# Rotation by 90 degrees: store sizes at the start and at the end of the store stretch

One core of a Trainium2 chip. The metric is the device time of one execution in microseconds (us). MB in the kernel's sizes means 1,048,576 bytes; GB/s and the bytes of the profile are decimal.

## The reference

```python
def reference(x):                       # x: (32, 3, 256, 256) float32
    return np.rot90(x, k=-1, axes=(-2, -1)).astype(np.float32)
```

Each of the 96 images of 256 x 256 numbers is turned clockwise. 25.17 MB are read and 25.17 MB are written; there is no arithmetic.

## The kernel before

The images are handled in 12 slabs of 2 MB. All of the input fits on the core, so each slab has a buffer of its own (`units[n]`), and slab n is turned into the buffer of slab n - 1, whose content is used up by then. Slab 0 has no predecessor: it is turned into `turned0` in PSUM and copied back to the last buffer at the end by ScalarE. VectorE does all the turning, two transposes for each slab; all transfers are issued from one queue, that of the sync engine (SP). The line numbers of the profile refer to the lines marked here.

```python
    for n in range(n_slabs):            # all 24 loads of 1 MB are issued first
        for i in range(I):              # I = 2
            if n in (0, last):
                nc.sync.dma_start(out=units[n][:, i], in_=ld8_v[n][:, i])            # L63
            else:
                nc.sync.dma_start(out=units[n][i::I]..., in_=ld16_v[n, i])           # L65

    for n in range(n_slabs):
        t_in, t_out = units[n], units[n - 1] if n else turned0
        if n in (0, last):
            for i in range(I):
                ...                     # each transpose makes one half of the slab
                nc.vector.transpose(out=dst[:, :, ::-1, ::-1], in_=src)              # L73
        else:
            for h in range(2):          # each transpose writes into both halves
                ...
                nc.vector.transpose(out=dst[:, cs], in_=src[:, cs])                  # L79

        if n == 1:                      # 128 KB, 896 KB, 1 MB
            nc.sync.dma_start(out=st_v[n][:, 0, :W], in_=t_out[:, 0, :W])            # L82
            nc.sync.dma_start(out=st_v[n][:, 0, W:], in_=t_out[:, 0, W:])            # L83
            nc.sync.dma_start(out=st_v[n][:, 1], in_=t_out[:, 1])                    # L84
        elif n in (2, 3):
            for i in range(I):
                nc.sync.dma_start(out=st_v[n][:, i], in_=t_out[:, i])                # L87
        elif n:
            nc.sync.dma_start(out=st_v[n], in_=t_out)                                # L89

    for i in range(I):
        nc.scalar.copy(out=units[last][:, i], in_=turned0[:, i])                     # L92
    nc.sync.dma_start(out=st_v[0], in_=units[last])                                  # L93
```

## Time and profile before

| | before |
|---|---|
| median of the first 3 runs | 123.54 us (123.51 to 123.78) |
| span of the profiled execution | 122.3 us |
| DMA queue, share of the 16 engines' span | 97.8% |
| rate in most slices | 429 GB/s |
| VectorE busy | 93.3 us (76%) |
| last transfer issued | 101.27 us |

VectorE's 76% looks high, but it ends at about 99 us while the transfers go on for another 21 us. Look at the chain that ended last, on the page of the kernel before (share of the span by engine, then by line):

```profile
DVE 47%; issue 27%; DMA 4%; DVEq 3%; ACT 2%
DVE u L79 37%; DVE turned L73 6%; DMA u<-in_x_dram 4%; DVE u L73 3%; DVEq L119 3%; ACT u L92 2%
```

It gives VectorE nearly half of the span and the transfers 4%.

### The profile page before, as it was taken

The numbers are of one execution on the slowest core, as the hardware profiler recorded it, in microseconds if no ns is written. First come the engines' busy times: TensorE is split into PE (matmuls) and PEld (weight loads), VectorE is DVE, ScalarE is ACT, GpSimd is POOL, SyncE is SP. The second block draws the span as 40 slices with busy tenths as digits, with TensorE's granted clock in tenths as the row PEclk, the third lists the DMA queues.
The fourth block names the chain that finished last, engine by engine and source line by source line (L and its number), as shares of the span: only waits on it lengthen the run. The fifth ranks groups of instructions, "written<-read, shape, count | busy, mean of one in ns | idle before, by whom it ended". The sixth has DMA issues, their size and how long they took to land.

```text
span 122.3 us, 138 instructions
## 1 busy us (share of the span) xinstructions
DVE 93.3 (76%) x24; ACT 5.0 (4%) x3; POOL 0.2 (0%) x4
## 2 busy tenths in 40 slices
DVE  0199999999999999999999999999999940000000
ACT  0000000000000000000400000000000641000000
POOL 0000000000000000000000000000000000000000
DMA  3999999999999999999999999999999999999994
GB/s 118 418 450 429 429 429 429 429 429 429 429 429 429 429 429 429 429 429 391 359 413 429 429 429 426 429 421 429 429 429 429 429 429 429 429 429 426 429 429 180
DMA packets 5632, 50.33 MB, mean 412 GB/s; under 512 B 640, under 2 KB 768, under 8 KB 896
## 3 DMA queue, kind: packets, MB, share of 16 engines
q1 hardware_dynamic: 5632, 50.33, 97.8%
HBM read 25.17 MB, written 25.17 MB: 412 GB/s over the span
## 4 chain that ended last, share of the span: by engine, by line
DVE 47%; issue 27%; DMA 4%; DVEq 3%; ACT 2%
DVE u L79 37%; DVE turned L73 6%; DMA u<-in_x_dram 4%; DVE u L73 3%; DVEq L119 3%; ACT u L92 2%
## 5 line engine op out<-in xcount | busy, mean ns | idle before, releaser
L79 DVE STREAM_TRANSPOSE u<-u 128x2048 f32<-128x2048 f32 x20 | 78.0, 3949 | 0.3
L73 DVE STREAM_TRANSPOSE turned<-u 128x2048 f32<-128x2048 f32 x2 | 7.6, 3828 | 5.6 <-DMA u<-in_x_dram 5.6
L73 DVE STREAM_TRANSPOSE u<-u 128x2048 f32<-128x2048 f32 x2 | 7.7, 3953 | 0.0
L92 ACT COPY u<-turned 128x2048 f32<-128x2048 f32 x2 | 3.7, 1866 | 36.5 <-DVE u L73 36.5
L92 ACT ACT_TABLE_LOAD x1 | 1.3, 1283 | 59.7 <-DMA u<-in_x_dram 59.7
L108 POOL MEMSET const-bfloat16-1.0<- 128x1 bf16 x1 | 0.1, 102 | 0.0
L108 POOL MEMSET const-uint8-127<- 128x1 uint8 x1 | 0.1, 102 | 0.0
L108 POOL MEMSET const-float32-0.0<- 128x1 f32 x1 | 0.1, 99 | 0.2 <-issue 0.2
L108 POOL MEMSET const-float32-1.0<- 128x1 f32 x1 | 0.1, 99 | 0.0
## 6 DMA issues: line engine op xcount, KB each, us to landing
u<-in_x_dram SPq DMA_DIRECT2D x24, 1024.0 KB, 19.6
out_dram<-u SPq DMA_DIRECT2D x9, 2048.0 KB, 23.0
out_dram<-u SPq DMA_DIRECT2D x5, 1024.0 KB, 17.7
out_dram<-u SPq DMA_DIRECT2D x1, 896.0 KB, 17.8
out_dram<-u SPq DMA_DIRECT2D x1, 128.0 KB, 18.3
```

What stands on the lines that cost most here:

```text
L73: nc.vector.transpose(out=dst[:, :, ::-1, ::-1], in_=src)
L79: nc.vector.transpose(out=dst[:, cs], in_=src[:, cs])
L92: nc.scalar.copy(out=units[last][:, i], in_=turned0[:, i])
L108: nc = _bacc.Bacc("TRN2", target_bir_lowering=False, num_devices=1)
L119: with _tile.TileContext(nc) as tc:
```

## The change

Large stores where the store stretch begins, small ones where it ends, with the number of transfers kept at 40. The likely intent: 2 MB stores carry less handling, and halves at the end can start as soon as their data is ready, so that less is left when the last piece of computing is over.

```diff
-        elif n in (2, 3):
+        elif n == last:
             for i in range(I):
                 nc.sync.dma_start(out=st_v[n][:, i], in_=t_out[:, i])
         elif n:
@@
     for i in range(I):
         nc.scalar.copy(out=units[last][:, i], in_=turned0[:, i])
-    nc.sync.dma_start(out=st_v[0], in_=units[last])
+        nc.sync.dma_start(out=st_v[0][:, i], in_=units[last][:, i])
```

## The prediction

> **What bounds the kernel now.** I read the page first, its rows for the 40 slices and for the DMA queue, because the kernel has no arithmetic beyond moving data:
>
> ```profile
> DMA  3999999999999999999999999999999999999994
> GB/s 118 418 450 429 429 429 429 429 429 429 429 429 429 429 429 429 429 429 391 359 413 429 429 429 426 429 421 429 429 429 429 429 429 429 429 429 426 429 429 180
> ...
> q1 hardware_dynamic: 5632, 50.33, 97.8%
> HBM read 25.17 MB, written 25.17 MB: 412 GB/s over the span
> ```
>
> The 16 DMA engines are busy for 97.8% of the span and move 429 GB/s in nearly every slice, loads first, stores after. 50.33 MB at 429 GB/s is 117.3 us. The span is 122.3 us, so only 5.0 us can be lost anywhere. The same row says where. A slice is 122.3/40 = 3.06 us. Slices 0 and 1 fall short by (311 + 11)/429 of a slice, 2.3 us, the start. Slices 18 to 20 (391, 359, 413), where the last loads give way to the first stores, fall short by (38 + 70 + 16)/429 of a slice, 0.9 us. The last slice falls short by 249/429 of one, 1.8 us, the end. That is all of it: 117.3 + 2.3 + 0.9 + 1.8 = 122.3 us. The kernel is bound by the transfers. The chain of waits on the page names VectorE with 47%, and is misleading here: it follows dependencies back from the last instruction, and a queue that is merely full isn't a dependency.
>
> Second, the timeline of the end, to see when work is ready and when it is issued (columns: start, length, engine, line, operation, names, count):
>
> ```profile
> 87.66 3.91 DVE L79 STREAM_TRANSPOSE u<-u 128x2048 f32<-128x2048 f32 x1
> 91.59 8.15 SPq L89 DMA_DIRECT2D out_dram<-u  x2
> 91.60 7.75 DVE L73 STREAM_TRANSPOSE u<-u 128x2048 f32<-128x2048 f32 x2
> 95.60 1.87 ACT L92 COPY u<-turned 128x2048 f32<-128x2048 f32 x1 [34.62 <-DVE u L73]
> 99.38 1.87 ACT L92 COPY u<-turned 128x2048 f32<-128x2048 f32 x1 [1.92 <-DVE u L73]
> 101.27 0.37 SPq L93 DMA_DIRECT2D out_dram<-u  x1
> ```
>
> The reader is to see that all computing is over at 101.25 us and the very last transfer is issued at 101.27 us, 21 us before the end. What happens in those 21 us, in windows (columns: stretch, its length, busy time of DVE, ACT and POOL, clock, DMA share, GB/s):
>
> ```profile
> 67.60:77.40 9.80, 9.73 (x4) 0.00 (x0) 0.00 (x0) 1.00 1.01 426
> 77.40:87.20 9.80, 9.77 (x3) 0.00 (x0) 0.00 (x0) 1.00 1.01 428
> ...
> 106.80:116.60 9.80, 0.00 (x0) 0.00 (x0) 0.00 (x0) 1.00 1.01 428
> 116.60:120.00 3.40, 0.00 (x0) 0.00 (x0) 0.00 (x0) 1.00 1.01 429
> 120.00:121.20 1.20, 0.00 (x0) 0.00 (x0) 0.00 (x0) 1.00 0.46 191
> ```
>
> The queue drains a backlog at full rate up to 120.0 us, ebbs away within about 1 us, and then come the final waits. The two slabs of the first window (67.6 to 77.4) are the ones stored in four 1 MB pieces; the next windows hold 2 MB stores. Both run at the same rate, 426 against 428.
>
> Third, the waits of the DMA queue, to see what paces the issues:
>
> ```profile
> SPq L65 <- DMA u<-in_x_dram: 25.5, 13, 2.0
> SPq L89 <- DVE u L79: 20.7, 4, 7.4
> ...
> SPq L87 <- DMA u<-in_x_dram: 8.3, 4, 2.1
> ```
>
> The four 1 MB stores that the change merges (L87) did not wait for VectorE. They waited for loads to land. From issue to landing the page gives 19.6 us for a load, and 1.049 MB at 429 GB/s takes 2.44 us: 8 transfers are in flight, and each issue waits for the transfer eight before it. The waits of L65 have the same form.
>
> **What the Trainium skill says.** "DMA: Bandwidth & Descriptors", section Where 436 GB/s comes from, puts the ceiling of a core's 16 DMA engines at 435 GB/s; the trace agrees, 429 sustained. The same page, Rules for kernel authors, asks for at least 1 MiB per DMA for full bandwidth. Every store that the change touches is 1 or 2 MB before and after, so both sides of it satisfy the rule, and the trace shows no difference between the two sizes. "Perfetto Trace Analysis", section DMA Optimizations, says of splitting: "If DMA engines are generally idle, splitting DMAs into smaller sections may allow the overall task to complete sooner." Here they are not idle at the place where the change splits, so its condition is not met.
>
> **The change part by part.**
>
> (a) Slabs 2 and 3: four stores of 1 MB become two of 2 MB. Removed: two issues of 0.33 us on the sync queue (timeline: 332 ns each), which lie beside a full queue and cost nothing. Bytes and rows of 8 KB stay as they are. Rate: if 426 against 428 were real and not the cut of the windows, it would be worth 0.5% of 9.8 us, 0.05 us. Both halves of such a slab become ready together (each transpose of L79 writes into both halves), so merging delays nothing.
>
> (b) Numbering. With two fewer stores early, every store of slabs 4 to 10 is issued one or two places further forward in the window of eight. Its data decides then: the waits of L89 for VectorE. Slabs 4 to 6 go out a few us sooner, into a queue that is already full. Cost and gain 0.
>
> (c) Slab 11: one 2 MB store becomes two of 1 MB. The first half is ready when the first L73 transpose ends, at about 95.5 us in place of 99.35 us. But when does the queue get to it? The bytes end at about 120.7 us; slabs 11 and 0 are the last two, 2.097 MB / 429 GB/s = 4.89 us each. So slab 11 begins to move at about 110.9 us and slab 0 at 115.8 us. Slab 11 has been ready for 11.5 us by then. Earlier by 3.9 us in the queue is later by nothing at the end: gain 0.
>
> (d) Slab 0: the same. Its second half is ready at 101.25 us as before, its first at 97.5 us but behind slab 11 in program order, so issued at about 99.8 us. Slack until 115.8 us: 14.5 us. Gain 0. The two extra issues, 0.33 us each, lie within the slack.
>
> (e) The window at the end. Forty transfers before and after. The last waits for the 32nd: before that was the store of slab 4, after it is that of slab 6. Stores start landing at about 62.7 us, so slab 6 lands at about 62.7 + 6 x 4.89 = 92 us, 9 us before the 40th wants to issue at 101.3 us. No new wait.
>
> (f) The end itself: the last transfer is 1 MB, not 2 MB. The ebb of about 1 us is the spread of the 16 engines, and they run through the same descriptors. I put 0.0, give or take 0.1 us.
>
> Sum: 0 with about 0.1 us either way, 123.5 us.
>
> **The rivals.**
>
> *Transition.* The dip of 0.9 us at slices 18 to 20 lies just where stores begin, and larger stores could help or worsen it. For it: the issues of slabs 2 and 3 (52.3 to 60 us) lie there. Against: the transfers that actually move then are the last loads and the three pieces of slab 1, which don't change. Were all of it won, 122.65 us; doubled, 124.4 us.
>
> *Queue room.* One 2 MB issue at 68.08 us took 2.31 us on the sync queue where others take 0.37 (timeline of the queue), so the queue seems to have a limit of outstanding work. With 2 MB stores from slab 2 on, this stall will come earlier, in the stretch from 57 to 68 us. If a stalled issue held back transfers, each would cost up to 2 us and the time would be 124 to 126 us. Against: in the stretch of the 2.31 us stall the DMA engines kept their 429 GB/s, since the stall means that the queue is full.
>
> *False dependency at the end.* If the second copy of ScalarE had to wait until the first half store of slab 0 has landed (about 118.5 us, the same tile), then 1.87 us of copy, some 2.4 us of transfer and the start of a transfer come after it: about 126 to 127 us. Against: the halves of a tile are kept apart already; the first copy runs at 95.60 us while VectorE still reads the other half of that tile (91.60 to 99.35 us).
>
> *A faster end.* The tail being the bound, earlier halves would win up to 3.8 us, 119.7 us. The 21 us of backlog after the last issue speak against it.
>
> **Range and chances.** The three runs before lie between 123.51 and 123.78 us. Predicted 123.5 us; the range 123.1 to 124.0 us holds this scatter, a few tenths of the transition either way, and a chip a little different. Two per cent are 2.5 us. Only the first rival can win anything and it can't win as much; faster 0.01. The false dependency or stacked stalls could lose it; slower 0.02. Same 0.97.
>
> **What would show it.** In the profile of the changed kernel: DMA share near 97.8% and 429 GB/s in all slices but the same three places; the sync queue's waits for VectorE moved to earlier stores; long issues (over 1 us) in the stretch 57 to 68 us without a dip beside them; the first half of slab 11 issued near 95.6 us and the last transfer still near 101.3 us, 20 us before the end. I am wrong if ScalarE's second copy starts later than about 100 us, if slices 18 to 22 change by more than a few per cent, or if the rate falls below 429 while the queue has work.

## The result, and the profile after

The changed kernel took 123.93 us (median of 6 runs, 123.80 to 124.30). The kernel before, with three runs more beside it, took 123.85 us (median of 6, 123.51 to 124.09). The ratio is 1.0016 with a 95% interval of 0.9993 to 1.0038: the same. Even that 0.16% hangs on the first three runs of the kernel before (mean 123.61 us): its three later runs have a mean of 123.99 us, the changed kernel's six one of 124.00 us. Two more sets of runs gave 0.9986 and 1.0002.

The page of the changed kernel, its DMA rows (busy tenths and GB/s in 40 slices, then the queue):

```profile
DMA  3999999999999999999999999999999999999994
GB/s 78 426 445 429 429 429 440 418 429 434 424 429 429 429 429 429 429 429 413 389 405 426 429 429 429 429 429 429 429 426 429 429 429 426 426 429 426 429 429 174
...
q1 hardware_dynamic: 5632, 50.33, 97.9%
```

The picture is the old one: 429 GB/s nearly everywhere, and less at the start, in slices 18 to 20 and at the end. The dip in the middle is somewhat shallower than before (413, 389, 405 against 391, 359, 413) and the start somewhat worse (78 against 118). Those two differ between executions of one and the same kernel, and here they nearly cancel.

The end of the changed kernel in its timeline (start, length, engine, line, operation, names, count):

```profile
91.75 0.37 SPq L89 DMA_DIRECT2D out_dram<-u  x1
91.75 7.75 DVE L73 STREAM_TRANSPOSE u<-u 128x2048 f32<-128x2048 f32 x2
95.75 4.13 SPq L87 DMA_DIRECT2D out_dram<-u  x2
95.75 1.87 ACT L92 COPY u<-turned 128x2048 f32<-128x2048 f32 x1 [34.82 <-DVE u L73]
99.54 1.86 ACT L92 COPY u<-turned 128x2048 f32<-128x2048 f32 x1 [1.92 <-DVE u L73]
99.97 2.49 SPq L93 DMA_DIRECT2D out_dram<-u  x2
```

The change does what it was meant to do. The first half of slab 11 is issued at 95.75 us, where the whole slab used to wait until 99.38 us. The second copy starts at 99.54 us, right after its transpose, so it waits for no store. It buys nothing, because the queue is busy with older work; here are the windows of the same trace after the last issue (stretch, length, busy time of DVE, ACT and POOL, clock, DMA share, GB/s):

```profile
106.70:116.50 9.80, 0.00 (x0) 0.00 (x0) 0.00 (x0) 1.00 1.01 428
116.50:119.90 3.40, 0.00 (x0) 0.00 (x0) 0.00 (x0) 1.00 1.01 426
119.90:121.10 1.20, 0.00 (x0) 0.00 (x0) 0.00 (x0) 1.00 0.46 191
```

Full rate to 119.9 us and about 1.2 us of ebbing away, as before.

And here is the chain that ended last on the page of the changed kernel:

```profile
DMA 52%; DVE 16%; issue 10%; DVEq 3%; ACT 2%; SPq 0%
DMA u<-in_x_dram 38%; DMA out_dram<-u 14%; DVE u L79 13%; DVE u L73 3%; DVEq L119 3%; ACT u L92 2%; SPq L63 0%; SPq L83 0%
```

From VectorE 47% to DMA 52% at the same time. It isn't the change that did this: two later profiles of the same changed kernel have DVE 47% with DMA 4%, and DVE 40% with DMA 20%. With 20 us of work in the queue, small differences seem to decide which dependency the chain follows back (argued, not tested). Neither version is a measurement of what bounds the kernel; the rate of the queue is.

### The profile page after: what moved, and what is told of

It is laid out like the page before. It is cut to its first block, busy times and chain, and to the rows that moved or that the text cites. A ratio compares the mean times of both kernels' runs of the same rounds, so it can differ in the third digit from the quotient of the medians.

```text
span 122.2 us, 140 instructions
## 1 busy us (share of the span) xinstructions
DVE 93.5 (76%) x24; ACT 5.0 (4%) x3; POOL 0.2 (0%) x4
## 3 DMA queue, kind: packets, MB, share of 16 engines
q1 hardware_dynamic: 5632, 50.33, 97.9%
## 4 chain that ended last, share of the span: by engine, by line
DMA 52%; DVE 16%; issue 10%; DVEq 3%; ACT 2%; SPq 0%
DMA u<-in_x_dram 38%; DMA out_dram<-u 14%; DVE u L79 13%; DVE u L73 3%; DVEq L119 3%; ACT u L92 2%; SPq L63 0%; SPq L83 0%
## 5 line engine op out<-in xcount | busy, mean ns | idle before, releaser
L73 DVE STREAM_TRANSPOSE turned<-u 128x2048 f32<-128x2048 f32 x2 | 7.6, 3829 | 5.7 <-DMA u<-in_x_dram 5.7
L73 DVE STREAM_TRANSPOSE u<-u 128x2048 f32<-128x2048 f32 x2 | 7.8, 3954 | 0.0
```

## The experiments

Theory: the transfers bound both kernels, 1 MB and 2 MB stores run at one rate, and the last slabs are ready some 10 us before the queue gets to them. So each part of the change is worth nothing, and only a drained queue would make the halves worth something.

Rivals: a part costs or wins a little, and the other hides it; the turn from loads to stores depends on store sizes; stalled issues hold transfers back; the end hangs on VectorE after all.

Beyond the first comparison there were 18 runs, of 14 kernels, all with correct results. The ratio is always to the kernel before in the same set.

| run | ratio | 95% interval | median us |
|---|---|---|---|
| after_again | 0.9986 | 0.9970 to 1.0002 | 123.66 |
| after_third | 1.0002 | 0.9988 to 1.0016 | 123.71 |
| merge_only | 1.0021 | 1.0003 to 1.0040 | 124.12 |
| merge_again | 1.0022 | 1.0006 to 1.0038 | 123.91 |
| merge_third | 1.0012 | 0.9999 to 1.0025 | 123.79 |
| tail_only | 1.0015 | 1.0000 to 1.0030 | 124.02 |
| tail_again | 1.0007 | 0.9992 to 1.0022 | 123.87 |
| before_again | 1.0005 | 0.9990 to 1.0020 | 123.82 |
| all_1mb | 1.0010 | 0.9990 to 1.0031 | 124.16 |
| all_2mb | 1.0014 | 0.9998 to 1.0031 | 123.86 |
| table_early | 1.0002 | 0.9987 to 1.0017 | 123.71 |
| late2_before | 0.9994 | 0.9978 to 1.0011 | 123.58 |
| late2_after | 1.0011 | 0.9995 to 1.0026 | 123.78 |
| late3_before | 1.0360 | 1.0333 to 1.0388 | 128.30 |
| late3_after | 1.0155 | 1.0128 to 1.0181 | 125.76 |
| late5_before | 1.1573 | 1.1538 to 1.1609 | 143.32 |
| late5_after | 1.1383 | 1.1367 to 1.1399 | 140.75 |
| late5_order | 1.1262 | 1.1232 to 1.1292 | 139.48 |

### The whole change, and each part alone

after_again and after_third are the changed kernel. The parts are small edits of the kernel before.

```diff
 merge_only:
-        elif n in (2, 3):
-            for i in range(I):
-                nc.sync.dma_start(out=st_v[n][:, i], in_=t_out[:, i])
 tail_only:
-        elif n in (2, 3):
+        elif n in (2, 3, last):
 ...
-    nc.sync.dma_start(out=st_v[0], in_=units[last])
+        nc.sync.dma_start(out=st_v[0][:, i], in_=units[last][:, i])
```

> The changed kernel once more, beside the two parts of its change. Theory (the transfers bound both kernels and every touched store waits in a full queue): ratio to the kernel before within 0.997 to 1.003. Rival (the two extra issues and the smaller pieces at the end cost a little, as the first measurement of 1.0016 hints): ratio above 1.0015 with an interval that leaves out 1.

> Only slabs 2 and 3 merged to one 2 MB store each, 38 transfers. Theory: ratio 0.997 to 1.003, 0 us. Rival (2 MB stores near the turn from loads to stores help or hurt there): up to 0.9 us either way, ratio 0.993 or 1.007, shown by slices 18 to 22.

> Only the last two slabs split in halves, 42 transfers. Theory: ratio 0.997 to 1.003, because the halves wait more than 10 us in the queue. Rival (an earlier start of the last stores shortens the end): 2.4 to 3.8 us less, ratio about 0.97 to 0.98. Rival (two more transfers cost their handling): 0.2 to 0.6 us more.

In this first set the parts lay at 1.0021 and 1.0015 with intervals at or just above 1, and the whole at 0.9986. Parts that cost 0.2% each can't make a whole that is faster, unless they undo each other. So the parts ran again, beside the kernel before against itself:

> The kernel before against itself. Theory (ratios of 0.998 to 1.002 here are scatter): it strays from 1 by up to 0.002, perhaps with an interval that nearly leaves out 1. Rival (the parts have a true cost): within 0.0005 of 1, with the repeated parts at 1.0015 to 1.002 beside it.

> The merge of slabs 2 and 3 alone, repeated. Theory: no fixed sign, 0.998 to 1.002. Rival (a true cost of 0.2%): 1.0015 to 1.0025 again.

> The split of the last two slabs alone, repeated. Theory: no fixed sign, 0.998 to 1.002. Rival (a true cost of 0.15%): 1.001 to 1.002 again.

The kernel before against itself gave 1.0005, the split alone 1.0007. But the merge gave 1.0022 again, against what I expected of scatter. So the merge and the whole change ran side by side once more:

> The merge alone a third time. If it has a true cost: 1.0015 to 1.0025. If scatter: anywhere from 0.998 to 1.002, and not apart from the changed kernel beside it by more than 0.002.

> The changed kernel a third time. Theory (no effect): 0.998 to 1.002. If the split gives back what the merge costs: 0.999 to 1.001 while the merge alone stands at 1.0015 to 1.0025.

1.0012 and 1.0002, intervals overlapping. The whole change is worth nothing: 1.0016, 0.9986 and 1.0002 have a mean of 1.0001. The merge alone may cost some 0.2%, about 0.2 us: its three results have a mean of 1.0018, two of three intervals leave out 1, and they reach up to 1.0040. That isn't settled, and no profile shows where such a cost would lie. From the landing of slab 1 to the landing of the last transfer (each taken as the mean of its 16 parts in the trace) the stores take 53.89 us in the kernel before and 53.86, 53.84 and 53.85 us in the three runs of the merge. The changed kernel, which contains the merge, has 53.87, 53.85 and 53.89 us. What does differ between executions comes earlier: from the landing of the third to last load to that of slab 1 it is 10.02 to 10.56 us over the kernels with this division of slab 1, and 10.16, 10.18 and 10.56 us for three executions of the changed kernel alone.

### All stores small, all stores large

```diff
 all_1mb:                                  # 49 transfers
-        elif n in (2, 3):
+        elif n > 1:
 ...
-    nc.sync.dma_start(out=st_v[0], in_=units[last])
+        nc.sync.dma_start(out=st_v[0][:, i], in_=units[last][:, i])
 all_2mb:                                  # 36 transfers
-        if n == 1:
-            ...                           # the three pieces of slab 1
-        elif n in (2, 3):
-            ...
-        elif n:
+        if n:
             nc.sync.dma_start(out=st_v[n], in_=t_out)
```

> Every store after slab 1 in 1 MB halves, 47 transfers, so only 8 MB can be outstanding in place of 16 MB. Theory: same rate, 429 GB/s, ratio 0.997 to 1.003; time from issue to landing falls to about 19.6 us for all stores. Rival (each transfer has a cost of its own): seven more transfers than before show it, at 0.1 us each 0.7 us, ratio 1.006.

(The count there is wrong: the kernel has 24 loads and 25 stores, 49 transfers, nine more than before.)

> Every store 2 MB, slab 1 too, 36 transfers. Theory: ratio 0.997 to 1.003. Rival (queue room: a stalled issue holds transfers back): long issues of over 1 us from 47 to 65 us, with a dip of the GB/s row beside them, 1 to 3 us more.

1.0010 and 1.0014, with 49 and 36 transfers: neither the number of transfers nor their size matters by more than the 0.3% that the two intervals leave open. The stretch of stores after slab 1 took 53.91 and 53.85 us. The page of the kernel with 1 MB stores has the transfers by kind (names, count, size, median us from issue to landing):

```profile
u<-in_x_dram SPq DMA_DIRECT2D x24, 1024.0 KB, 19.6
out_dram<-u SPq DMA_DIRECT2D x23, 1024.0 KB, 19.5
```

19.5 us is again eight times 2.44 us, so 8 MB in the queue is still plenty. The other extreme is the hard test of the queue's room. In its timeline, asked for one issue at a time, three of the early issues are long (L82 there is the store of a whole slab):

```profile
52.25 2.06 SPq L82 DMA_DIRECT2D out_dram<-u  x1
...
54.70 4.23 SPq L82 DMA_DIRECT2D out_dram<-u  x1
...
60.35 3.85 SPq L82 DMA_DIRECT2D out_dram<-u  x1
```

The sync queue is held for 10 us in all where three normal issues (0.37 us) would take 1.1 us. The row of GB/s on the same page:

```profile
GB/s 75 427 443 430 430 430 430 430 430 430 430 430 430 430 430 430 430 430 411 384 430 427 430 430 427 430 422 430 422 427 430 430 427 424 427 424 430 430 430 191
```

A slice is 3.05 us, so the first long issue lies in slice 17, which has 430. Slices 18 and 19 have the usual dip, and slice 20, with most of the third stall in it, again 430, where the kernel before had 413 and no long issue. The second long issue lies in the dip itself. Asked for the three stretches of stall (52.3 to 54.3, 54.7 to 58.9 and 60.4 to 64.2 us), this trace has 401, 410 and 403 GB/s; the kernel with 1 MB stores, without an issue over 1 us there, has 393, 406 and 406. A stalled issue doesn't hold transfers back: the queue rival falls.

### The dip in the middle

ScalarE loads its table at 59.7 us, in the middle of the dip, so it was a suspect. In table_early a tiny copy into a place that is overwritten later brings the load forward to 0.72 us.

```diff
+    nc.vector.memset(turned0[:, 0, :1], 0.0)
+    nc.scalar.copy(out=turned0[:, 0, 1:2], in_=turned0[:, 0, :1])
```

> The kernel before with a tiny ScalarE copy at the start, so that the load of ScalarE's table lies there and not at 59.7 us, beside the dip where stores begin. If the table load makes the dip, slices 18 to 20 come to 429 and the time falls by 0.3 to 0.9 us. If the turn from loads to stores makes it (my theory), the dip stays and the ratio is 0.998 to 1.002.

The row of GB/s on its page keeps the dip, at 414, 387 and 416:

```profile
GB/s 94 425 433 430 430 436 430 430 430 425 430 425 430 430 430 430 430 430 414 387 416 432 428 428 428 428 430 422 430 428 428 430 428 428 425 430 428 428 430 199
```

Ratio 1.0002. The table load isn't the cause. It stands in every page at the place where the loads end and the stores begin to move, and that is as far as the runs go: no run took the turn itself away.

### A late last slab: how much slack is there, and what are halves worth without it

The strongest test of "the queue doesn't get there before" is to use the slack up. Each transpose of the last slab is done two, three or five times over (R), with the same result, in the kernel before and in the changed one.

```diff
-                nc.vector.transpose(out=dst[:, :, ::-1, ::-1], in_=src)
+                for _ in range(R if n == last else 1):
+                    nc.vector.transpose(out=dst[:, :, ::-1, ::-1], in_=src)
```

In the built kernels the repetitions seem to alternate between the halves, though the source has them one half after the other: ScalarE's first copy, which waits for the first half, starts one transpose before the last one ends (at 110.49 us with three repetitions, the second copy at 114.27 us). So the first half is always about 3.8 us ahead of the second, however long the delay. The lines of these kernels lie one further on than in the kernel before: L74 is its L73.

> The kernel before, with each transpose of the last slab done twice (same result), so that its data is ready 7.9 us later, at about 107.3 us. Theory: the queue reaches slab 11 only at about 111 us[...], so 0 us, ratio 0.997 to 1.005. Rival (the end hangs on VectorE's last transpose, as the chain of waits has it): 7.9 us more, ratio 1.064.

> The changed kernel with each transpose of the last slab done twice. Theory: 0 us, as for the kernel before with the same delay. Rival (the end hangs on the last transpose): 7.9 us more less the worth of the halves, about 4 to 5.5 us more.

> The kernel before, each transpose of the last slab done three times: data ready at about 115.3 us, after the queue has drained at about 111.6 us. Theory: from the issue at 115.3 us about 7.1 us to the landing of slab 11, 4.9 us more for slab 0, 127.3 us for the last landing in place of 121.5: 5.9 us more, ratio 1.048. Rival (no slack, hangs on the last transpose): 15.8 us more.

> The changed kernel with the same delay. Theory: the first half of slab 11 is ready at about 103.5 us and moves before the queue drains, so 1 MB less is left after 115.3 us: 2.4 us less than the kernel before with the same delay, ratio about 1.028. Rival (splitting at the end is worth nothing even with an empty queue): the same as the kernel before with the delay, ratio 1.048.

> The kernel before, each transpose of the last slab done five times: data ready at about 131.1 us, queue empty for 20 us. Theory: 131.1 + 7.1 + 4.9 = 143.1 us for the last landing, 21.7 us more, ratio 1.175.

With two repetitions, the timeline of the kernel before has

```profile
91.78 15.26 DVE L74 STREAM_TRANSPOSE u<-u 128x2048 f32<-128x2048 f32 x4
```

The data is ready at 91.78 + 15.26 = 107.04 us, 7.7 us later than the 99.35 us of the kernel before, and both kernels take the same time as ever (0.9994 and 1.0011). A delay of 7.7 us on the engine to which the chain gives 47% costs nothing. With three and five, the kernel before shows these lines in its timelines, one trace each:

```profile
91.46 22.77 DVE L74 STREAM_TRANSPOSE u<-u 128x2048 f32<-128x2048 f32 x6
```

```profile
91.47 37.78 DVE L74 STREAM_TRANSPOSE u<-u 128x2048 f32<-128x2048 f32 x10
```

The data is ready at 114.23 and 129.25 us, 14.88 and 29.90 us later than in the kernel before. The time grew by 128.30 - 123.78 = 4.52 us and 143.32 - 123.78 = 19.54 us. Each pair leaves the same difference, 10.4 us: that is the slack. (The times are medians. With the spans of the profiled executions, 122.3, 126.5 and 141.5 us, the same sum gives 10.7 us.) My expectation for three repetitions, 5.9 us, was too high by two of its terms: the transposes in a row came to 22.77/6 = 3.80 us each, not 3.95, so the data was ready 1.1 us sooner than I had put, and a store of 2 MB issued into an empty queue landed after 6.50 us, not 7.1. The same two terms make up the miss with five repetitions, 19.5 us for an expected 21.7.

Now the queue is empty when the last slab comes, and the same change does pay: 125.76 us against 128.30 us with three repetitions, 2.5 us, which is 1 MB at 429 GB/s (2.44 us). The size was as expected, the way not quite: the first half was issued at 110.50 us, not 103.5, just before the queue ran dry. That the split works where its condition holds, and is worth nothing in the original, is the positive half of the proof.

> The changed kernel, each transpose of the last slab done five times, its own order of issues. Theory: 1 MB of the four moves before the second half of slab 11 is ready, so 2.4 us less than the 143.3 us of the kernel before with the delay: about 140.8 us, ratio 1.137. Rival (the split alone does it, the order nothing): as the reordered kernel, 139.5 us, ratio 1.126.

> The changed kernel with the same delay of five transposes, and the first half of slab 0 issued right after the first half of slab 11, ahead of its second half. Theory: with the order of the change 2.4 us would be won against the kernel before with the delay; with this order a second 1 MB moves in the empty stretch, so 4.9 us are won in all, 16.8 us more than the kernel before, ratio 1.136. If only the split counts and not the order: 19.3 us more, ratio 1.156.

```diff
 late5_order, against the changed kernel:
         elif n == last:
             for i in range(I):
                 nc.sync.dma_start(out=st_v[n][:, i], in_=t_out[:, i])
+                nc.scalar.copy(out=units[last][:, i], in_=turned0[:, i])
+                nc.sync.dma_start(out=st_v[0][:, i], in_=units[last][:, i])
```

With five repetitions the halves win 143.32 - 140.75 = 2.6 us, and the better order 143.32 - 139.48 = 3.8 us. (late5_after ran in another set of rounds than the other two; the ratios, 1.1573, 1.1383 and 1.1262, say the same.) The 4.9 us that I expected of the order are not reached. Why, the windows show, asked in each trace for the same stretches (length, DVE, ACT, POOL, clock, DMA share, GB/s). The kernel before with the delay:

```profile
111.60:126.90 15.30, 15.30 (x5) 1.39 (x1) 0.00 (x0) 1.00 0.00 0
126.90:131.00 4.10, 2.35 (x1) 2.19 (x2) 0.00 (x0) 1.00 0.23 96
131.00:136.00 5.00, 0.00 (x0) 0.15 (x1) 0.00 (x0) 1.00 1.02 419
```

The changed kernel with the delay:

```profile
126.90:131.00 4.10, 2.30 (x1) 2.18 (x2) 0.00 (x0) 1.00 0.70 288
```

The changed kernel with the delay and the other order:

```profile
126.90:131.00 4.10, 2.37 (x1) 2.19 (x2) 0.00 (x0) 1.00 1.01 416
```

While the second half is being turned, the DMA engines stand nearly still in the first, have one piece to move in the second (a share of 0.70) and are busy without a gap in the third. They can't be more than busy, and they have something to do only from the moment when the first half is ready, 3.8 us ahead of the second. So the gain, in the cases run, is the smaller of two numbers: what the pieces issued early take to move (2.4 us for one, 4.9 us for two), and the head start of their data (3.8 us).

## Why the prediction was right or wrong

**What bounds it: right.** 97.9% and 429 GB/s in the changed kernel, and no layout of stores changed the stretch of stores.

**(a) and (b), the merge and the numbering: right in what they do, with a remainder.** The issues moved as described: the sync queue's waits of L89 for VectorE grew from 20.7 us in four waits to 26.9 us in five. The worth of 0 us holds for the change as a whole. For the merge alone a cost of some 0.2 us, against my 0 to 0.05 us of gain, stays possible.

**(c) to (f), the halves at the end, the window of eight and the ebb: right.** The first half of slab 11 was issued at 95.75 us (predicted about 95.6), the last issue began at 101.43 us (predicted 101.3), and no wait on the 32nd transfer appeared. The last 1.2 us of moving had 191 GB/s before and after. The slack was put at 11.5 us and measured as 10.4 us. The prediction compared the time when data is ready with the time when bytes move and left out what lies between. In the kernel before with five repetitions the issue was at 129.28 us, and the first packet after it in the trace starts at 130.16 us: 0.9 us. 11.5 - 0.9 = 10.6 us comes close.

**The rivals.** *Transition*: it stayed as it was, within what executions differ by. Taken at its word, the prediction's own sign of being wrong, slices 18 to 22 changing by more than a few per cent, did appear: 359 became 389, 8% more. But the sign was set too fine: three profiles of the changed kernel have 389, 401 and 319 in that slice. The other sign, a rate below 429 with work in the queue, was no better, since single slices of 421 and 426 stood in the kernel before already. *Queue room*: wrong in its detail and right in its verdict. I expected long issues from 57 to 68 us; only one came, 1.11 us at 62.59 us, and the 2.31 us issue of the kernel before at 68.08 us became an ordinary one (0.37 us; the other 2 MB issues of the kernel before took 0.37 to 0.77 us, not all 0.37). In its place the two last issues took 1.20 and 1.03 us. What decides the length of an issue is open; that stalls of 10 us in all cost no more than that kernel's interval leaves open (ratio up to 1.0031) is shown by the kernel with 2 MB stores only. *False dependency*: it didn't occur. *A faster end*: it comes only with an empty queue.

**The step that failed: the base, that is, going from the sum to the number.** The mechanism gave a change of 0 us; the term that it was added to was mis-sized. The prediction took "The three runs before lie between 123.51 and 123.78 us. Predicted 123.5 us", that is, the median of three runs as the level of the kernel, and gave "this scatter, a few tenths of the transition either way, and a chip a little different" up to 124.0 us. Its sum was made from another execution: the span of 122.3 us belongs to a run of the kernel before that took 124.06 us, by its result file. Adding 0 us to that gives 124.06 us, above the upper end of the range. So the mechanism said 0 us, and the number said something else: against the 123.85 us of the kernel before in the same comparison, 123.5 us is a gain of 0.3%, for which no step of the prediction argues. Measured, the kernel before had medians of 123.85, 123.90, 123.73, 123.78, 123.66 and 123.76 us in the sets, and single runs from 123.45 to 124.39 us. In the first comparison alone, its first three runs have a mean of 123.61 us and its next three one of 123.99 us, with nothing changed in the kernel; why is open. A level of 123.8 us with 123.4 to 124.4 us for single runs would have been the right size. The median of the changed kernel, 123.93 us, fell just inside the range; two of its six runs, 124.15 and 124.30 us, fell outside.

## What to carry to other kernels

Before you split or merge transfers, look at how long the queue goes on working after its last issue: while it was 20 us behind, as here, earlier or smaller stores changed nothing that these runs can tell from scatter, and even the busiest engine had 10 us of slack. With an empty queue, halves at the end were worth the smaller of the time of the pieces that can go early and the head start of their data, so mind the order of the issues too. And predict a change as a ratio to a level with its true scatter: three runs that agree within 0.3 us did not show the level.

## What the Trainium skill lacked or had wrong

- "Perfetto Trace Analysis", DMA Optimizations, says that splitting may help if the DMA engines are idle. The runs agree, and add the size: 0 us with the queue behind, 2.5 us for one early piece of 1 MB with an empty queue, and 3.8 us in place of 4.9 us for two pieces, since the data's head start was 3.8 us.
- "DMA: Bandwidth & Descriptors", section Measured, lists 341 GB/s for a load of 1 MB (issued from another engine). For a row of 1 MB stores on this chip the page has no figure: here 1 MB stores back to back in a full queue ran at 426 to 430 GB/s, as fast as those of 2 MB, and 49 transfers took the time of 36.
- "Perfetto Trace Analysis", DMA Instruction — HWDGE (DVE, Sync), says that a DMA instruction's length in the profile isn't the movement of its data. The runs agree (issues of 0.37 us, landings 17.2 to 28.9 us after them, for the 2 MB stores of the kernel before) and add the reverse: an issue can take 2.06 to 4.23 us where others take 0.37 us, with the DMA rate unharmed. No page has a time or a limit for such long issues, and these runs leave open what decides them.
- No page has the turn from loads to stores: two or three slices of 3 us below 429 GB/s (391, 359 and 413 in the kernel before, 411 and 384 with 2 MB stores alone), in every kernel here whatever the store sizes. By the sum of the prediction it costs 0.9 us in the kernel before and (18 + 45)/429 of a slice, 0.4 us, with 2 MB stores alone; but that executions of one kernel differ as much (10.16 to 10.56 us for the same stretch of the changed kernel) forbids crediting the store sizes.
- No page says where the run-to-run scatter of a transfer-bound kernel comes from. In the profiled executions without a gap in the queue, the stretch of stores differs by 0.07 us (53.84 to 53.91 us) and the stretch of the turn before it by 0.54 us (10.02 to 10.56 us), so little of the scatter arises in the stretch of stores. What causes it is open. Sets of four runs spread over 0.21 to 0.44 us without a gap and over 0.03 to 0.27 us with one (three and five repetitions). That the gap swallows the scatter is a reading that these overlapping ranges don't show.
